# A selection's place in VectorE's queue, and four gates copied out by ScalarE: one Trainium2 core

## The chip, the cores and the metric

The kernel runs on one core of one Trainium2 chip. The metric is the time of one execution in device microseconds; lower is better. Each version is given by the median of several runs, and one further execution of each was profiled.

## The reference, cut to what matters

Two layers over 512 tokens and 1024 channels, all in float32. The part that the change touches is the mixing half of a layer:

```python
h = rms_norm(x); z = h @ w_in           # one projection, its columns shared out:
qa, ka, va, qi, ki, wi, cq, ckv, kr, ga, gb = split_cols(z)
# mixer A: an indexer scores every earlier key, the best 128 of each query are attended
score = einsum(relu(qi . ki), wi);  sel = top_k(score, 128)
y_a = softmax(qa . ka[sel] * scale + bias[sel]) @ va[sel]
# mixer B: latent attention
qb = rms_norm(rope(rms_norm(cq) @ b_w_uq));  kb, vb = from rms_norm(ckv) @ b_w_ukv
y_b = softmax(qb . kb * scale + chunk_mask) @ vb
# merge
gate_a = sigmoid(ga + b_gate[:1024]);  gate_b = sigmoid(gb + b_gate[1024:])
x = x + (gate_a * (y_a @ w_proj_a) + gate_b * (y_b @ w_proj_b)) @ w_out
```

A feed-forward half follows and is not touched.

## The kernel before, in words

Activations lie transposed: channels on the 128 partitions, 512 tokens along the free dimension. Each float32 operand of a product is split into a high part (rounded by ScalarE) and a low part (the difference, mostly by VectorE), and a product is three matmuls. A weight tile of the fixed plan is loaded by SP's queue; ScalarE makes its high part, and its low part comes from VectorE or, for some tiles (gb, ga, kv and uq among them), from a ScalarE copy with the sign turned and an adding DMA on POOL's queue.

**How the order comes about.** The Python program is a set of generators that are advanced in turn. `fl.fill(1)` advances the projections (`mix_dense`) by about three matmuls (a "fill") and moves a clock by one; `later(n, f)` runs `f` when the clock has gone on by n; `flush` runs all that is pending. So the program traces instructions in an order, and this order is their priority. A planner then puts each engine's instructions in a queue at compile time: it goes through time with its own costs and, whenever an engine is free, takes the ready instruction traced earliest. An instruction traced much later, whose inputs are there, can so be placed ahead. On the chip each engine works its queue off in that fixed order. `tc.add_manual_dep(a, b, no_sync)` adds an order to the planner (a behind b) without a semaphore. Tiles are buffers of named pools: PSUM has banks D (2, projections), L (3, mixer B's keys, values, queries and all scores), T (2, transposes), Y (1).

**The stage around the change**, once a layer (layer 0 at about 40 to 340 us of the span, layer 1 at about 800 to 1100):

1. The indexer's queries and keys, then the latents ckv and cq. `index_scores` gives three score tiles `sc` (query blocks 3, 2, 1 with 512, 384, 256 keys).
2. `top_k` (L1036, L1043) on VectorE: 16 rounds. A round takes the 8 largest of each tile (`V.max`, three instructions, one a tile) and strikes them out (`V.match_replace`, three more, each with a short load): 96 steps, each dependent only on steps of its own tile. Three instructions at the end (L1047) write `sel`. POOL adds `sel` to the relative-position bias when mixer A begins (`bias_a`, L1115), and `scores_a` reads the sum (L1134).
3. While `fl.until("b0", side_0)` runs, the fills are gb's gates 0 to 3 (24 matmuls each, eight fills) and then `attn_b(0)`: four blocks of keys and values (L856), four of queries (L893). Each fill is followed by RATE_0 = 1 selection steps. `evac_gate` empties a gate's D bank (L702: `gb = p * row` on VectorE, where `row` is the norm's reciprocal root spread over the tile). Of a value block, ScalarE copies the keys, casts the values and squares the keys, and VectorE makes the values' low part (L315, `vb<-L,vb`): with that the L bank is free. The scaling of the keys (L880) and of the queries (L924) by VectorE comes 22 ticks after their norms, and the transposes (L1149) need it.
4. Mixer B: eight heads, each `scores_b` (VectorE maximum L1167, ScalarE exponential L369), scaling by VectorE (L1063), transposes L1074, products L1081. `each_b` advances the projections meanwhile (`attn_b(1)`, gb 4 to 7, then `attn_a(0)`), and the selection by RATE_T = 0.2 steps a call. What is left of the selection is traced behind mixer B.
5. Mixer A, eight heads, with ga's gates among the fills; then the sigmoids (L369 on gb, ga), the projections pb and pa, and the merge (L944, L1337, L1338).

An option `PK`, off here, tied the first maximum of a round behind the latest gate eviction or row maximum (`tables["v"]`); an option `GBL`, off, had all gb gates copied by ScalarE and multiplied just ahead of the sigmoids.

Of the kernel before, what the change touches and what calls it, by code (L numbers as in the profile page):

```python
# [10 lines left out]
F32 = mybir.dt.float32  # L11
# [4 lines left out]
OP = mybir.AluOpType  # L16
# [23 lines left out]

RATE_B = [0.85, 0.55, 0.75, 0.55]
RATE_A = [0.95, 1.05, 0.65, 0.95]
RATE_T = 0.2
LAG_S = 22
LAG_T = 4
GAP_B = 12
# [6 lines left out]
POOL = ''  # L53
# [9 lines left out]
PBO = 0  # L63
VL = 0
TAIL = 1
TAIL_3 = 3
PK = 0
RATE_0 = 1
DL = ['gb', 'ga', 'uv', 'ug', 'kv', 'uq']
DN1 = []  # L70
DN2 = []
# [3 lines left out]
SU2 = '12'  # L75
PCH = 2000
GA_0 = 0
GBL = 0
LAG_D = [2, 4, 5, 7, 8, 10, 12]
WPOOL = []  # L80
WMOD = 1
# [165 lines left out]
def trunk(ctx: ExitStack, tc: tile.TileContext, xT, wd, vecs, bias, rot_n, outT):  # L247
# [33 lines left out]
    V, A, G = nc.vector, nc.scalar, nc.gpsimd  # L281
# [5 lines left out]
    def later(n, f):  # L287
        if n == 0:
            f()
        else:  # L290
            pending.append((clock[0] + n, f))
# [17 lines left out]
        split_into(h, o, src, scale, lag)  # L309
        return h, o  # L310

    def split_into(h, o, src, scale=None, lag=1):
        if scale is None:
            A.copy(h, src)
            later(lag, lambda: V.tensor_tensor(out=o, in0=src, in1=h.bitcast(F32), op=OP.subtract))  # L315
        else:
            A.activation(h, src, AF.Copy, scale=scale)
            later(lag, lambda: V.scalar_tensor_tensor(o, src, scale, h.bitcast(F32), op0=OP.mult, op1=OP.subtract))
# [45 lines left out]
    no_sync = mybir.DependencyInfo(mybir.DependencyClass.NoSync, mybir.DependencyReason.DATA)  # L364
# [204 lines left out]
    done = set()  # L569
    late = []  # L570

    def mix_dense(l, nrm):
# [122 lines left out]

        def evac_gate(name, m, p):
            g = slot(name)
            if name == "gb" and GBL and not PBO:
                A.copy(g, p)
                late.append((g, nrm.row))  # L700
            else:
                tables["v"] = V.tensor_tensor(out=g, in0=p, in1=nrm.row, op=OP.mult)  # L702
            st[name][m] = g
# [129 lines left out]
        def attn_b(g):  # L833
# [12 lines left out]
            while len(st.get("ckvl", ())) < 2:  # L846
                yield
            h, o = W.get("kv", g)
            for t in range(4):
                ts = slice(t * 128, (t + 1) * 128)  # L850
                p = bank(BB)
                xs = [(st["ckvh"][k][:, ts], st["ckvl"][k][:, ts]) for k in range(2)]
                seq = ([(x, h, k) for k in range(2) for x in xs[k]] + [(xs[k][0], o, k) for k in range(2)] if "k" in LO
                       else [q for k in range(2) for q in ((xs[k][0], h, k), (xs[k][1], h, k), (xs[k][0], o, k))])
                for n, (x, w, k) in enumerate(seq):
                    mm(p, lhsT=x, rhs=w[:, k * 512:(k + 1) * 512], start=n == 0, stop=n == 5, skip_group_check=True)  # L856
                    if n == 2:
                        yield
                if t == 3:
                    W.ahead()  # L860
                p = p.rearrange("p (h c) -> p h c", c=64)
                A.copy(k4[t][:, :, 0:64], p[:, 0:4])
                v = vb[t].rearrange("p (h c) -> p h c", c=128)
                split_into(v[:, :, 0:64], v[:, :, 64:128], p[:, 4:8])
                squares(p[:, 0:4], ssk[:, t], 64)
                yield

            def keys():
                m = small("mk", [4, 4])
                V.tensor_tensor(out=m, in0=ssk, in1=st["sskr"][:, :, None].to_broadcast([128, 4, 4]), op=OP.add)  # L870
                V.tensor_scalar(m, m, 1.0 / 96, EPS, op0=OP.mult, op1=OP.add)
                r = rsqrt(m, [4, 4])

                def scale():
                    for t in range(4):
                        G.tensor_tensor(out=k4[t][:, :, 64:96],
                                        in0=st["kr"][:, t:t + 1, :].to_broadcast([128, 4, 32]),
                                        in1=r[:, t, :, None].to_broadcast([128, 4, 32]), op=OP.mult)
                        G.tensor_copy(k4[t][:, :, 96:100], late_k[:, t:t + 1, :].to_broadcast([128, 4, 4]))
                        (G if "K" in POOL else V).tensor_tensor(out=k4[t][:, :, 0:64], in0=k4[t][:, :, 0:64],  # L880
                                        in1=r[:, t, :, None].to_broadcast([128, 4, 64]), op=OP.mult)
                later(LAG_S, scale)
            later(3, keys)
# [32 lines left out]
            def queries():  # L916
                m = small("mq", [4, 4])
                V.scalar_tensor_tensor(m, ssq, 1.0 / 96, st["epscq"][:, :, None].to_broadcast([128, 4, 4]),
                                       op0=OP.mult, op1=OP.add)
                r = rsqrt(m, [4, 4])  # L920

                def scale():
                    for t in range(4):
                        (G if "Q" in POOL else V).tensor_tensor(out=q4[t][:, :, 0:96], in0=q4[t][:, :, 0:96],  # L924
                                        in1=r[:, t, :, None].to_broadcast([128, 4, 96]), op=OP.mult)
                later(LAG_S, scale)
            later(3, queries)
            st["b", g] = (qn, kn, vb)
# [100 lines left out]
    def top_k():  # L1029
        def low():  # L1030
            return tc.high_priority(offset=-PT) if PT else ExitStack()
        m8 = {i: small("m8", [8]) for i in (1, 2, 3)}
        for _ in range(TOPK // 8):
            for i in (3, 2, 1):
                with low():
                    ins = V.max(out=m8[i], in_=st["sc"][i][:, :128 * (i + 1)])  # L1036
                if PK and i == 3 and "v" in tables:
                    tc.add_manual_dep(ins.ins, tables["v"].ins.name, no_sync, reason="spread")
                yield
            for i in (3, 2, 1):  # L1040
                s = st["sc"][i][:, :128 * (i + 1)]
                with low():
                    V.match_replace(out=s, in_to_replace=m8[i], in_values=s, imm_value=TAKEN)  # L1043
                yield
        for i in (3, 2, 1):
            w = 128 * (i + 1)
            V.tensor_scalar(sel[:, SEL0[i]:SEL0[i] + w], st["sc"][i][:, :w], TAKEN, BIG, op0=OP.not_equal,  # L1047
                            op1=OP.mult)
            yield
# [182 lines left out]
    for l in range(DEPTH):  # L1232
# [10 lines left out]

        fl.fill(GAP_I)
        weave([index_scores()], lambda: fl.fill(1))
        tk = top_k()

        def side_tk(n):
# [6 lines left out]
        due = [0.0]  # L1255

        def side_0():
            due[0] += RATE_0
            side_tk(int(due[0]))
            due[0] %= 1  # L1260

# [4 lines left out]
        def mixer(name, scores, turn, v, each, group):  # L1266
# [6 lines left out]
            for h in range(8):  # L1273
                if h == (3 if turn else 4):
                    fl.until(group + "1")
                    flush()
                each.at(h)
                if turn:
                    P = sb.tile([128, 1280], F32, name=nm("P"), tag="P", bufs=WB[2])
                else:  # L1280
                    P, ahead = (ahead if h else first_a), (bias_a(h + 1) if h < 7 else None)
# [26 lines left out]
                     lambda h: lambda j: st["va"][j][h // 4][:, (h % 4) * 128:(h % 4 + 1) * 128], each_a, "a")  # L1308
        fl.until("ga")
        gb = st["gb"]  # L1310
        for g, row in late:
            V.tensor_tensor(out=g, in0=g, in1=row, op=OP.mult)
        late.clear()
        for m in range(0 if PBO else 8):
            table(AF.Sigmoid, gb[m], gb[m], bias=vc(l, V_GATE + 8 + m))

# [334 lines left out]
```

## Time and profile before

| what | value |
|---|---|
| median of 3 runs | 1537.66 us (1537.4 to 1538.77) |
| the profiled execution | 1536.24 us, its span 1534.5 us |
| busy, share of the span | TensorE 99%, VectorE 73%, ScalarE 62%, POOL 26% |
| granted TensorE clock | 1.00 |
| selection maxima (L1036) | 96, the first at 52.6 us, the last at 929.0 us |
| `sel` written (L1047) | first at 175.1 us, last at 937.3 us |
| gb evictions by VectorE (L702) | 16, median 680 ns |

The page gives busy time and idle time for each engine; idle time of an engine matters only where TensorE waits for it. A row of a group reads: line, engine, operation, tiles out<-in, shapes, xcount, then busy us, mean ns of one, and idle us ahead of it with what ended it. A row by stretch reads: stretch, its length, then busy us and (xcount) of PE, PEld, DVE, ACT, POOL, and at the end clock, DMA share and GB/s; where one line was asked for, only its own engine's number stands there. A row of a tile reads: line, engine, operation, tiles, xcount, shortest/median/longest ns, first and last start.

### The profile page before, as it was taken

The numbers are of one execution on the slowest core, as the hardware profiler recorded it, in microseconds if no ns is written. First come the engines' busy times: TensorE is split into PE (matmuls) and PEld (weight loads), VectorE is DVE, ScalarE is ACT, GpSimd is POOL, SyncE is SP. The second block draws the span as 40 slices with busy tenths as digits, with TensorE's granted clock in tenths as the row PEclk, the third lists the DMA queues.
The fourth block names the chain that finished last, engine by engine and source line by source line (L and its number), as shares of the span: only waits on it lengthen the run. The fifth ranks groups of instructions, "written<-read, shape, count | busy, mean of one in ns | idle before, by whom it ended". The sixth has DMA issues, their size and how long they took to land.

```text
span 1534.5 us, 23946 instructions
## 1 busy us (share of the span) xinstructions
PE 1525.7 (99%) x8658; PEld 1335.7 (87%) x8658; DVE 1124.4 (73%) x2305; ACT 946.3 (62%) x1553; POOL 396.3 (26%) x578
## 2 busy tenths in 40 slices
PE   9999999999999999999999999999999999999999
PEld 8887999888888898889998889998888888988899
DVE  7899988666476693547979999886674857835586
ACT  7756668773577536664557576687635765456642
POOL 2343012400011442124602520223001115311364
PEclk9999999999999999999999999999999999999999
DMA  7464124733488438873454641356436783488732
GB/s 247 108 158 119 53 86 113 190 118 116 128 191 190 104 117 218 194 177 90 152 171 112 159 107 56 104 134 174 129 97 147 182 189 91 149 197 197 181 99 91
DMA packets 73575, 216.29 MB, mean 141 GB/s; under 512 B 8432, under 2 KB 11504, under 8 KB 73456
## 3 DMA queue, kind: packets, MB, share of 16 engines
q1 hardware_dynamic: 54592, 149.08, 30.7%
q0 software_dynamic: 18432, 65.28, 22.8%
q8 instruction: 68, 1.11, 0.3%
q14 instruction: 51, 0.42, 0.1%
q10 hardware_dynamic: 432, 0.40, 0.1%
HBM read 141.06 MB, written 4.19 MB: 95 GB/s over the span
## 4 chain that ended last, share of the span: by engine, by line
PE 86%; DVE 11%; ACT 2%; issue 1%; DMA 0%; SPq 0%; DVEq 0%; ACTq 0%
PE D L535 37%; PE T L535 15%; PE D L558 7%; PE L L1446 5%; PE T L1446 4%; PE D L1446 3%; DVE sc L1043 2%; PE Y L1081 2%; DVE m L1036 2%; PE Y L1446 2%; PE T L1074 2%; PE L L535 2%; PE L L336 1%; PE L L335 1%; PE L L728 1%
## 5 line engine op out<-in xcount | busy, mean ns | idle before, releaser
L182 ACT CAST wh<-wr 128x1024 fp32r<-128x1024 f32 (+2 forms) x205 | 211.3, 1034 | 163.7 <-PE D L535 73.8
L211 POOL DMA_DIRECT2D wl<-wr x128 | 110.7, 874 | 630.2 <-ACT wl L210 591.9
L535 PE MATMUL D<-hxh,wh 128*128 128x512 f32 (+1 forms) x440 | 174.0, 396 | 0.0
L535 PE MATMUL D<-hxl,wh 128*128 128x512 f32 (+1 forms) x440 | 172.8, 393 | 0.0
L210 ACT ACTIVATE wl<-wr 128x1024 fp32r<-128x1024 f32 (+2 forms) x128 | 132.2, 1035 | 48.1 <-PE D L535 25.9
L200 ACT CAST wh<-wr 128x896 fp32r<-128x896 f32 x88 | 82.6, 942 | 102.4 <-POOL wr L224 56.2
L1115 POOL TENSOR_TENSOR P<-M,sel 128x128 f32<-128x128 f32 (+1 forms) x64 | 53.4, 889 | 271.2 <-DMA M<-in_bias_dram 150.2
L535 PE MATMUL D<-hxh,wl 128*128 128x512 f32 (+1 forms) x440 | 117.8, 393 | 0.0
L224 POOL TENSOR_TENSOR wr<-wr 128x256 f32<-128x256 f32 x88 | 101.0, 1151 | 57.9 <-DVE wr L223 41.9
L558 PE MATMUL D<-wh,hxh 128*128 128x256 f32 x384 | 113.8, 297 | 0.0
L205 DVE TENSOR_TENSOR wl<-wr,wh 128x896 fp32r<-128x896 f32 x88 | 101.9, 1161 | 10.2 <-ACT wh L200 4.3
L558 PE MATMUL D<-wl,hxh 128*128 128x256 f32 x384 | 109.3, 285 | 0.0
L558 PE MATMUL D<-wh,hxl 128*128 128x256 f32 x384 | 108.4, 283 | 0.0
L535 PE MATMUL D<-hrl,wh 128*128 128x512 f32 x256 | 99.6, 389 | 0.0
L535 PE MATMUL D<-hrh,wh 128*128 128x512 f32 x256 | 99.6, 389 | 0.0
L535 PE MATMUL T<-hrh,wh 128*128 128x512 f32 x256 | 99.6, 389 | 0.0
L535 PE MATMUL T<-hrl,wh 128*128 128x512 f32 x256 | 99.6, 389 | 0.0
L194 DVE TENSOR_TENSOR wl<-wr,wh 128x1024 fp32r<-128x1024 f32 x77 | 94.9, 1238 | 6.3 <-ACT wh L182 5.6
L535 PEld LDWEIGHTS D<-hxh,wh 128*128 128x128 f32 x440 | 82.9, 188 | 13.4 <-DVE gb L702 0.2
L535 PEld LDWEIGHTS D<-hxl,wh 128*128 128x128 f32 x440 | 82.9, 188 | 12.7
L535 PEld LDWEIGHTS D<-hxh,wl 128*128 128x128 f32 x440 | 80.2, 188 | 14.0
L1390 DVE SCALAR_TENSOR_TENSOR c<-T,vec,c 128x511 f32<-128x511 f32 x32 | 23.9, 748 | 89.1 <-ACT c L1387 89.1
(458 smaller groups left out, 4571.4 us busy)
## 6 DMA issues: line engine op xcount, KB each, us to landing
wr<-in_wd_dram SPq DMA_DIRECT2D x197, 512.0 KB, 3.8
wl<-wr POOLq DMA_DIRECT2D x120, 512.0 KB, 5.4
wr<-in_wd_dram SPq DMA_DIRECT2D x88, 256.0 KB, 2.6
x<-in_xT_dram SPq DMA_DIRECT2D x16, 256.0 KB, 5.2
M<-in_bias_dram SPq DMA_DIRECT2D x16, 256.0 KB, 4.0
wr<-in_wd_dram SPq DMA_DIRECT2D x7, 384.0 KB, 3.2
kah<-kah SPq DMA_DIRECT2D x16, 128.0 KB, 4.3
kal<-kal SPq DMA_DIRECT2D x16, 128.0 KB, 3.8
```

The source lines that it names most:

```text
L182: ins = self.nc.scalar.copy(h[:, :n], t[:, :n])
L194: eng.tensor_tensor(out=o[:, c], in0=t[:, c], in1=h[:, c].bitcast(F32), op=OP.subtract)
L200: self.nc.scalar.copy(h[:, :896], t[:, 128:1024])
L205: self.later(lag, lambda: self.nc.vector.tensor_tensor(out=o[:, :896], in0=t[:, 128:1024], in1=h[:, :896].bitcast(F32), op=OP.subtract))
L210: self.nc.scalar.activation(o, t, AF.Copy, scale=-1.0)
L211: self.nc.gpsimd.dma_start(o.bitcast(F32), t, accum_op=OP.add)
L224: g(2)(out=b[:, 6:8], in0=b[:, 0:3:2], in1=b[:, 3:6:2], op=OP.add)
L535: mm(p[:, t0:], lhsT=w, rhs=x[:, t0:], start=n == 0, stop=n == len(seq) - 1, skip_group_check=True)
L558: mm(pp[b][:, t, :], lhsT=x, rhs=w, start=n == 0 and half == 0 and t == 0, stop=n == 11 and half == 1, skip_group_check=True)
L1036: ins = V.max(out=m8[i], in_=st["sc"][i][:, :128 * (i + 1)])
L1115: G.tensor_tensor(out=P[:, P0[i]:P0[i] + w], in0=M[:, 512 - w:512], in1=sel[:, SEL0[i]:SEL0[i] + w], op=OP.add)
L1446: mm(p, lhsT=w, rhs=x, start=b0, stop=b1, skip_group_check=True)
```

## The change

- The selection (`PK = 1`): every maximum, of all three tiles, is placed behind the latest "hold" traced so far. A hold is the low part of a value block (`split_into(..., last=True)`), a key scaling or a query scaling of mixer B. It is cleared at the start of each layer's selection, so that maxima traced ahead of the first value block are free.
- Its rates: 1.55 steps a fill until the first value weight is taken up (`done.add("values")`), 0.5 from there until group 0 is through, 0.25 a call in mixer B.
- The gates gb 0 to 3 (`GBL = 4`): ScalarE copies the bank as it is; the multiplication with `row` is traced at the start of mixer A's heads 4, 5, 6 and 7, one each, on VectorE in SBUF. It was traced for all ahead of the sigmoids in the old option.

```diff
-RATE_T = 0.2
+RATE_T = 0.25
...
-PK = 0
-RATE_0 = 1
+PK = 1
+RATE_0 = 1.55
+RATE_1 = 0.5
...
-GBL = 0
+GBL = 4
+LATE_H = (4, 5, 6, 7)
...
-    def split_into(h, o, src, scale=None, lag=1):
+    def split_into(h, o, src, scale=None, lag=1, last=False):
         if scale is None:
             A.copy(h, src)
-            later(lag, lambda: V.tensor_tensor(out=o, in0=src, in1=h.bitcast(F32), op=OP.subtract))
+
+            def low():
+                ins = V.tensor_tensor(out=o, in0=src, in1=h.bitcast(F32), op=OP.subtract)
+                if last:
+                    tables["hold"] = ins
+            later(lag, low)
...
-            if name == "gb" and GBL and not PBO:
+            if name == "gb" and m < GBL:
                 A.copy(g, p)
                 late.append((g, nrm.row))
...
             h, o = W.get("kv", g)
+            done.add("values")
...
-                split_into(v[:, :, 0:64], v[:, :, 64:128], p[:, 4:8])
+                split_into(v[:, :, 0:64], v[:, :, 64:128], p[:, 4:8], last=True)
...
-                        (G if "K" in POOL else V).tensor_tensor(out=k4[t][:, :, 0:64], in0=k4[t][:, :, 0:64],
+                        tables["hold"] = V.tensor_tensor(out=k4[t][:, :, 0:64], in0=k4[t][:, :, 0:64],
...
-                        (G if "Q" in POOL else V).tensor_tensor(out=q4[t][:, :, 0:96], in0=q4[t][:, :, 0:96],
-                                        in1=r[:, t, :, None].to_broadcast([128, 4, 96]), op=OP.mult)
+                        tables["hold"] = V.tensor_tensor(
+                            out=q4[t][:, :, 0:96], in0=q4[t][:, :, 0:96], in1=r[:, t, :, None].to_broadcast([128, 4, 96]), op=OP.mult)
...
-                if PK and i == 3 and "v" in tables:
-                    tc.add_manual_dep(ins.ins, tables["v"].ins.name, no_sync, reason="spread")
+                if PK and "hold" in tables:
+                    tc.add_manual_dep(ins.ins, tables["hold"].ins.name, no_sync, reason="spread")
...
+        tables.pop("hold", None)
         tk = top_k()
...
-            due[0] += RATE_0
+            due[0] += RATE_1 if "values" in done else RATE_0
...
                 each.at(h)
+                if not turn and h in LATE_H:
+                    g, row = late.pop(0)
+                    V.tensor_tensor(out=g, in0=g, in1=row, op=OP.mult)
...
-        for g, row in late:
-            V.tensor_tensor(out=g, in0=g, in1=row, op=OP.mult)
-        late.clear()
```

## The prediction

> **What bounds the kernel now.** I read the page's totals first, then busy time by stretch, then what TensorE (PE) waited for, then the order on VectorE (DVE).
>
> ```profile
> span 1534.5 us, 23946 instructions
> PE 1525.7 (99%) x8658; PEld 1335.7 (87%) x8658; DVE 1124.4 (73%) x2305; ACT 946.3 (62%) x1553; POOL 396.3 (26%) x578
> ```
>
> PE is busy nearly throughout, so the change can gain only where PE waits or lose by making it wait: all of PE's idle time is 1534.5 - 1525.7 = 8.8 us. The stretches around the selection, layer 0 and then layer 1 (PE, PEld, DVE, ACT, POOL):
>
> ```profile
> 66.00:92.00 26.00, 26.00 (x121) 21.66 (x120) 26.00 (x76) 11.01 (x16) 5.15 (x7) 1.00 0.56 133
> 92.00:118.00 26.00, 24.59 (x119) 19.87 (x118) 26.00 (x92) 17.57 (x43) 17.89 (x52) 1.00 0.69 167
> 118.00:138.00 20.00, 19.38 (x104) 15.56 (x103) 19.74 (x59) 16.25 (x35) 10.30 (x26) 1.00 0.53 132
> 138.00:176.00 38.00, 37.84 (x254) 33.99 (x253) 37.78 (x91) 24.76 (x59) 0.00 (x0) 1.00 0.21 70
> 176.00:224.00 48.00, 47.57 (x376) 45.75 (x375) 41.96 (x99) 34.77 (x75) 0.00 (x0) 1.00 0.29 89
> 853.00:880.00 27.00, 26.43 (x130) 22.03 (x129) 27.00 (x95) 19.29 (x45) 17.88 (x52) 1.00 0.74 178
> 880.00:900.00 20.00, 19.56 (x107) 15.95 (x106) 20.00 (x64) 17.44 (x36) 10.38 (x26) 1.00 0.51 108
> 900.00:938.00 38.00, 38.00 (x255) 34.58 (x254) 37.40 (x88) 24.98 (x59) 0.00 (x0) 1.00 0.27 83
> 938.00:985.00 47.00, 46.58 (x368) 44.85 (x367) 40.81 (x94) 34.61 (x74) 0.00 (x0) 1.00 0.29 88
> ```
>
> VectorE has no idle time from 66 to 118 and hardly any until 176, and PE idles 1.41 + 0.62 = 2.03 us where mixer B's keys, values and queries are made (92 to 138), 0.57 + 0.44 = 1.01 us in layer 1. The clock is 1.00 everywhere. PE's waits by line and releaser (sum, times, longest): three rows of 92 to 138, two of 853 to 900, and one that fell in 138 to 176:
>
> ```profile
> PE L L856 <- DVE vb L315: 0.8, 2, 0.6
> PE L L1164 <- ACT P L369: 0.6, 1, 0.6
> PE L L893 <- DVE vb L315: 0.5, 1, 0.5
> PE T L1074 <- DVE P L1063: 0.4, 1, 0.4
> PE L L856 <- DVE vb L315: 0.4, 1, 0.4
> PE T L1074 <- DVE tbl L315: 0.2, 1, 0.2
> ```
>
> Four of the six large ones wait for a value eviction (vb). Why that was late stands in VectorE's order, and what a wait costs in PE's (start, duration; the last row is from the chain, 24 matmuls without a wait):
>
> ```profile
> 97.74 0.87 DVE L1036 MAX8 m<-sc 128x8 f32<-128x384 f32 x2
> ...
> 99.26 0.54 DVE L1043 MATCH_REPLACE8 sc<-m,sc 128x384 f32<-128x384 f32 x1
> 99.72 0.41 DVE L315 TENSOR_TENSOR vb<-L,vb 128x256 fp32r<-128x256 f32 x1
> ...
> 107.96 0.39 PE L535 MATMUL D<-hxl,wh 128*128 128x512 f32 x1
> 108.94 0.50 PE L856 MATMUL L<-wh,ckvh 128*128 128x512 f32 x1 [0.59 <-DVE vb L315]
> ...
> 430.52 5.44 PE D L535 x24
> ```
>
> The eviction at 99.72 sits behind 2.0 us of selection, all of it L1036 and L1043 from 97.74 on. The wait shown as 0.59 costs 108.94 - 107.96 - 0.23 (one pitch, 5.44 / 24) = 0.75 us: a shown wait plus 0.16, since a matmul's modelled end lies 0.16 after the next one's start. So the five rows (six waits) cost 0.8 + 0.6 + 0.5 + 0.4 + 0.4 = 2.7, plus 6 x 0.16, together 3.7 us. Idle time that these rows don't list, 2.03 + 1.01 - 2.7, adds 0.3. **At stake: 4.0 us.**
>
> **The tie.** Each selection maximum (L1036) may no longer stand on VectorE ahead of the latest value eviction, key scaling or query scaling traced before it. It adds no instruction and no semaphore: it is an order in VectorE's own queue. What I count along the generators: four gates and a step are 33 fills from the start of the wait for b0 to the first value weight. At 1.55 steps a fill some 50 steps are traced there (33 at rate 1), untied, and with the replacements of that round 54 may run freely. The 16 fills of group 0's values and queries add 8 at 0.5, mixer B's start until group 1's query scaling about 8 more at 0.25. So maxima 55 to 57 come behind group 0's last value eviction, 61 to 63 behind group 1's last one and its key scaling, and from 67 on all wait for group 1's query scaling, which stands at 138 now. So 66 steps are done by then. How many are now:
>
> ```profile
> 92.00:138.00 46.00, 8.34 (x16) 1.00 0.62 152
> 92.00:138.00 46.00, 8.94 (x30) 1.00 0.62 152
> 853.00:900.00 47.00, 10.34 (x19) 1.00 0.64 148
> 853.00:900.00 47.00, 10.93 (x37) 1.00 0.64 148
> 138.00:176.00 38.00, 4.09 (x8) 1.00 0.21 70
> 138.00:176.00 38.00, 5.28 (x18) 1.00 0.21 70
> 900.00:938.00 38.00, 2.44 (x5) 1.00 0.27 83
> 900.00:938.00 38.00, 3.57 (x12) 1.00 0.27 83
> ```
>
> (L1036, then L1043, in each stretch; L1043 has a load and a replacement to a step.) After 138 stand 8 + 9 = 17 steps, after 900 stand 5 + 6 = 11, so of 96 steps 79 and 85 are done ahead, and 79 - 16 - 15 = 48 and 85 - 19 - 18 = 48 when the values begin at 92 and 853. The tie moves 13 and 19 steps behind the query scaling. One step takes (8.34 + 8.94 + 10.34 + 10.93) / (16 + 15 + 19 + 18.5) = 0.563 us, so 7.3 and 10.7 us leave the stretch in which evictions queue. VectorE's load there falls to (45.7 - 7.3) / 46 = 84% and (47 - 10.7) / 47 = 77%. At 87% (41.96 of 48, 176 to 224) PE idled 0.43 us in 48, in waits for other things. I let all of the 4.0 us go; the lower bound is the vb waits of the one stretch with a direct cause, 0.5 + 0.16.
>
> What queues behind a waiting maximum: nothing on a semaphore, but VectorE now stands still where evictions aren't ready, and the selection ends later. In 138 to 176, beside 17 steps, one wait of 0.2 (0.36 in cost) fell to VectorE; layer 1's 11 steps show none. 32 steps more at 0.36 for 28 are 0.4 us, taken as a **loss of 0.4**. The bound of zero is layer 1; the upper end is the slower rival.
>
> **The gates.** Four of the eight gate evictions of a layer leave VectorE (680 ns, L702); ScalarE copies instead and VectorE multiplies in SBUF:
>
> ```profile
> L702 DVE TENSOR_TENSOR gb<-D,row x16: 665/680/694, 74.8 to 924.3; 128x512 f32<-128x512 f32 x16
> L1338 DVE TENSOR_TENSOR ga<-ga,gb x16: 682/686/693, 356.4 to 1138.5; 128x512 f32<-128x512 f32 x16
> L314 ACT CAST pth<-T 128x512 fp32r<-128x512 f32 x16 | 9.3, 582 | 0.4 <-PE T L1074 0.3
> ```
>
> A copy of this size costs ScalarE 582 ns: 4 x 0.58 = 2.3 us into a stretch where it has 26 - 11 = 15 us idle, so nothing, as long as the two D banks (5.44 us of matmuls each, by the chain's row of 24) cover a queue of two weight conversions. VectorE gets 4 x 0.68 = 2.7 us, worth 4.8 steps, so the free 54 are through when the values begin. The multiplication is traced at mixer A's heads 4 to 7, but nothing ties it: its inputs are ready from 75 us on, and the planner may put it into the holes that the tie makes. It costs as much as the eviction did (686 against 680 ns), so VectorE's total doesn't fall. In the crowded stretches 38.6 us of selection (the four numbers above) cost PE at most 4.0 us, 0.10 each. Eight late multiplications there, 5.5 us, would cost 0.6 at that rate; the 5.4 us that leave ahead of the values gain as much, which the 4.0 holds already. I take 0, which is right if the planner leaves them at or near mixer A's heads; bounds -0.6 and +0.6.
>
> The Trainium skill, Perfetto Trace Analysis, section Optimizing Scalar/DVE Operations, gives a VectorE access overhead of about 60 ns in SBUF and 125 ns in PSUM; by it each late multiplication would be an estimated 65 ns cheaper, 0.5 us of VectorE time in eight. The rows above show 686 against 680 ns, no gain, and the sum goes by the rows.
>
> The same PSUM banks, weights, matmuls and DMAs remain. POOL only loses a choice that was off (its list is empty), and neither SP's nor POOL's queue is passed by anything.
>
> **Sum.** -4.0 + 0.4 + 0 = -3.6 us. The profiled execution took 1536.24 us (its span plus 1.7), so it becomes 1532.6; the median of the runs is 1537.66, 1.4 higher, and I forecast **1534.1**.
>
> **Rivals.**
>
> *The wait moves* (same). With VectorE free, the next to be late is ScalarE, which empties the same L banks three times a tile (17.57 of 26 and 19.29 of 27 us busy), or POOL, whose rotations come ahead of the query scaling (17.89 of 26). Or the tie binds too late: VectorE must have passed the 50 untied steps when the first eviction is ready; it stood at 48, and the freed 4.8 steps leave a margin of three. Then half of 4.0 remains: -2.0 + 0.4, 1536.1.
>
> *The selection ends too late* (slower). Mixer A's first bias addition reads its result:
>
> ```profile
> 224.04 7.52 POOL L1115 TENSOR_TENSOR P<-M,sel 128x128 f32<-128x128 f32 x8 [93.69 <-DMA M<-in_bias_dram]
> 985.57 7.52 POOL L1115 TENSOR_TENSOR P<-M,sel 128x128 f32<-128x128 f32 x8 [91.49 <-PE T L1074]
> 230.45 0.28 DVE L1134 CUSTOM_DVE_ANT_0 P<-L,P 128x128 f32<-128x128 f32 x1
> ```
>
> The moved 7.3 + 10.7 = 18.0 us must fit into VectorE's idle time of 138 to 224 and 900 to 985: 0.22 + 6.04 and 0.60 + 6.19, 13.05 us, and half of the 6.4 us between the addition and its first reader, 3.2 a layer. With a share f of the idle time usable, the balance is 18.0 - 13.05 f - 6.4 - 4.0 = 7.6 - 13.05 f: a loss over 3.1 us below f = 0.34, none above 0.58. At f = 0.2 it is +5.0, 1542.7. For it: the order is fixed ahead, and an idle slot goes unused where no step stands. Against: 138 to 176 used 99% beside the selection. The Trainium skill, Perfetto Trace Analysis, section Identifying the Most-Contended Engine, says to speed up the engine with the highest occupancy; VectorE's work stays as it was here, and by that page this rival is the natural outcome.
>
> **How the numbers follow.** 0.2% is 3.1 us, about what a measurement here can tell from nothing. The forecast's case has 0.6 (from -1.5 to -7; 0.43 of it beyond -3.1), the moved wait 0.23 (0.04 beyond), the late selection 0.17 (0.15 beyond +3.1). Faster 0.47, same 0.38, slower 0.15. The range: 1530.5 takes in the 4.0, the 0.16 + 0.43 + 0.42 us of PE's idle time after 138, and 1 us a layer for another order of PE's work (its idle time differs by 1.0 between the layers); 1540.5 reaches halfway into the late selection. The forecast's own range is 1530.5 to 1536.
>
> **What would show it.** PE's rows "L856 <- DVE vb" and "L893 <- DVE vb" gone or under 0.3; fewer than 70 steps ahead of group 1's query scaling; VectorE idle above 5 us in 92 to 138; no gb eviction by L702 for the first four, a ScalarE copy instead; the result of the selection (sel) written at 195 to 225 instead of 175; the first bias addition still at 220 to 225, 985 less the gain in layer 1. I'm wrong if POOL's first addition waits for sel, if new PE waits for VectorE appear in 138 to 224, or if the late multiplications stand directly ahead of vb evictions.

## The result, and the profile after

The changed kernel takes 1547.37 us (median of 6 runs, 1545.47 to 1549.0), the kernel before 1537.75: ratio 1.0062, interval 1.0049 to 1.0075. It is 9.6 us slower where 3.6 us less were forecast. The profiled execution took 1549.0 us (before: 1536.24), so the traces below have to explain 12.8 us, of which 3 are the luck of the two executions. In the new kernel's line numbers the value eviction is L319, the key scaling L888, the query scaling L932, the selection L1044 and L1051, the products L1089, the late multiplication L1289.

```profile
span 1547.3 us, 23946 instructions
PE 1529.6 (99%) x8658; PEld 1335.9 (86%) x8658; DVE 1131.8 (73%) x2305; ACT 950.3 (61%) x1561; POOL 389.1 (25%) x578
```

The same 2305 VectorE instructions take 7.4 us more (1131.8 against 1124.4). Where the time went is seen from the lengths of the stages, each from a first matmul to the next stage's first, so that the work in them is the same: values to the end of mixer B, then mixer A, for both layers. First the kernel before, then the changed one (stretch, length, then busy us of PE, PEld, DVE, ACT, POOL):

```profile
90.30:217.00 126.70, 124.27 (x802) 110.39 (x801) 121.76 (x333) 91.10 (x204) 28.37 (x78) 1.00 0.37 102
217.00:336.90 119.90, 119.72 (x756) 106.52 (x754) 83.33 (x211) 90.93 (x185) 32.57 (x40) 1.00 0.48 131
853.80:978.40 124.60, 123.35 (x803) 110.81 (x802) 119.07 (x328) 92.52 (x205) 28.26 (x78) 1.00 0.39 103
978.40:1098.30 119.90, 119.72 (x755) 106.45 (x754) 83.16 (x211) 91.06 (x185) 33.66 (x40) 1.00 0.49 131
```

```profile
91.20:222.80 131.60, 125.51 (x803) 110.81 (x802) 125.03 (x331) 91.76 (x206) 28.50 (x78) 1.00 0.36 99
222.80:343.70 120.90, 120.04 (x754) 106.36 (x753) 83.17 (x211) 91.08 (x185) 32.75 (x40) 1.00 0.47 129
860.70:989.00 128.30, 124.16 (x803) 110.53 (x801) 122.87 (x325) 93.25 (x206) 26.67 (x78) 1.00 0.38 100
989.00:1111.10 122.10, 120.64 (x755) 106.45 (x754) 85.50 (x211) 91.02 (x185) 33.71 (x40) 1.00 0.49 129
```

The stretch with mixer B grew by 4.9 and 3.7 us, mixer A by 1.0 and 2.2 us. VectorE now stands idle there (131.60 - 125.03 = 6.6 us, 4.9 before), and TensorE waits more, mostly for it:

```profile
PE L L864 <- DVE vb L319: 3.3, 3, 1.2
PE Y L1089 <- DVE ptl L319: 1.9, 5, 0.6
PE L L1172 <- ACT P L376: 1.7, 2, 0.8
PE L L901 <- DVE vb L319: 1.6, 2, 0.8
PE T L800 <- DVE ptl L319: 1.4, 3, 0.7
PE T L1157 <- DVE qn L932: 0.9, 2, 0.5
```

The waits for value evictions, which the change was to remove, went from 1.7 to 4.9 us, and waits for the low parts of the probabilities (ptl), absent before, add 3.3. What stands ahead of the late evictions is in VectorE's order. Here are two places (start, duration):

```profile
93.41 0.41 DVE L1051 MATCH_REPLACE8 sc<-m,sc 128x256 f32<-128x256 f32 x1
93.73 2.49 DVE L1289 TENSOR_TENSOR gb<-gb,row 128x512 f32<-128x512 f32 x4
96.14 0.41 DVE L319 TENSOR_TENSOR vb<-L,vb 128x256 fp32r<-128x256 f32 x1
...
107.66 1.03 DVE L888 TENSOR_TENSOR kn<-kn,y 128x256 f32<-128x256 f32 x2
108.62 0.54 DVE L851 TENSOR_REDUCE ssq<-sqb 128x4 f32<-128x384 f32 x1
109.08 0.73 DVE L888 TENSOR_TENSOR kn<-kn,y 128x256 f32<-128x256 f32 x1
109.74 0.41 DVE L319 TENSOR_TENSOR vb<-L,vb 128x256 fp32r<-128x256 f32 x1
110.07 0.61 DVE L926 SCALAR_TENSOR_TENSOR mq<-ssq,ms 128x16 f32<-128x16 f32 x1
110.61 1.58 DVE L888 TENSOR_TENSOR kn<-kn,y 128x256 f32<-128x256 f32 x1
112.19 0.41 DVE L319 TENSOR_TENSOR vb<-L,vb 128x256 fp32r<-128x256 f32 x1
```

At 93.73 all four late multiplications, traced at mixer A's heads 4 to 7, stand ahead of group 0's first value eviction. At 107.66 three key scalings of group 0 stand ahead of group 1's first value eviction (none before), and the fourth, stretched to 1.58 us, ahead of its second. The tied steps left a hole, and the planner filled it with what was ready. A key scaling cost 0.41 us before; here POOL works beside it:

```profile
L880 DVE TENSOR_TENSOR kn<-kn,y x16: 409/411/547, 108.9 to 885.5; 128x256 f32<-128x256 f32 x16
```

```profile
L888 DVE TENSOR_TENSOR kn<-kn,y x16: 424/617/1585, 107.7 to 893.2; 128x256 f32<-128x256 f32 x16
L1055 DVE TENSOR_SCALAR sel<-sc x6: 263/348/421, 197.2 to 956.7; 128x512 bf16<-128x512 f32 x2, 128x384 bf16<-128x384 f32 x2, 128x256 bf16<-128x256 f32 x2
```

POOL's rotations, 0.32 us when alone, are stretched as well (start, duration):

```profile
106.32 0.31 POOL L919 TENSOR_TENSOR qn<-qn,rot 128x64 f32<-128x64 f32 x1
...
107.81 1.04 POOL L914 TENSOR_TENSOR rot<-qn,rotn 128x64 f32<-128x64 f32 x1
```

By the second row above (`sel`), the first part of the selection's result is written at 197 (in layer 0) and the last at 957 (in layer 1), instead of 175 and 937. That puts the last steps between mixer B's probabilities in its second half:

```profile
195.50 0.67 DVE L1051 MATCH_REPLACE8 sc<-m,sc 128x512 f32<-128x512 f32 x1
...
196.17 0.53 DVE L1051 MATCH_REPLACE8 sc<-m,sc 128x384 f32<-128x384 f32 x1
...
196.69 0.40 DVE L1051 MATCH_REPLACE8 sc<-m,sc 128x256 f32<-128x256 f32 x1
197.02 0.27 DVE L319 TENSOR_TENSOR ptl<-T,pth 128x128 fp32r<-128x128 f32 x1
...
197.35 0.33 PE L1089 MATMUL Y<-ptl,vb 128*128 128x128 f32 x1 [0.37 <-DVE ptl L319]
```

Three replacements, with their loads 1.5 us, stand ahead of the low part that TensorE's product waits for.

### The profile page after: what moved, and what is told of

Read it like the earlier page. It is cut to its first block, busy times and chain, and to the rows that moved or that the text cites. A ratio compares the mean times of both kernels' runs of the same rounds, so it can differ in the third digit from the quotient of the medians.

```text
span 1547.3 us, 23946 instructions
## 1 busy us (share of the span) xinstructions
PE 1529.6 (99%) x8658; PEld 1335.9 (86%) x8658; DVE 1131.8 (73%) x2305; ACT 950.3 (61%) x1561; POOL 389.1 (25%) x578
## 4 chain that ended last, share of the span: by engine, by line
PE 73%; DVE 7%; ACT 2%; issue 1%; DVEq 0%; ACTq 0%
PE D L542 33%; PE T L542 15%; PE L L1455 5%; PE T L1455 4%; PE D L565 3%; PE D L1455 3%; PE Y L1455 2%; PE L L542 2%; PE Y L1089 2%; PE T L1082 1%; DVE sc L1051 1%; DVE m L1044 1%; DVE sc L1032 1%; PE L L343 1%; PE L L342 0%
## 5 line engine op out<-in xcount | busy, mean ns | idle before, releaser
L226 POOL TENSOR_TENSOR wr<-wr 128x256 f32<-128x256 f32 x88 | 93.8, 1069 | 63.0 <-DVE wr L225 51.4
```

The source lines that it names most:

```text
L226: g(2)(out=b[:, 6:8], in0=b[:, 0:3:2], in1=b[:, 3:6:2], op=OP.add)
```

## The experiments

Two quantities from the traces help below. **Excess** is the sum, over the matmuls of a stretch, of the time from one start to the next less the usual time (40th percentile) of a matmul of that shape. **Steps behind** are the selection's maxima and replacements that stand in VectorE's queue behind group 1's last query scaling. Letters of theories are those of the expectation, or of its group, in which they stand. Times are medians of five rounds or more; the kernel before had 1536.96 to 1537.24 in these groups.

**Which part loses.** `e1_tie_alone`: the change without the ScalarE gates, so the tie with its new rates.

```diff
-GBL = 4
-LATE_H = (4, 5, 6, 7)
+GBL = 0
+LATE_H = ()
```

> The tie and its rates, with all gates evicted by VectorE as before the change. Theory H (the tie makes a hole on VectorE, and the late multiplications are planned into it ahead of the value evictions; these cost most of the loss): 2 to 5 us less than the changed kernel, 1542 to 1545. Theory T (the tie itself costs: key scalings and others fill the hole, the queue behind an eviction that is not ready stands still): as slow as the changed kernel, 1546 to 1548. Theory G (the gates' move costs, whatever the tie): as before the change, 1537 to 1539.

1547.52, ratio 1.0070 (1.0059 to 1.0081). `e2_gates_alone`: the gates without the tie, at the old rates (`PK = 0`, `RATE_T = 0.2`, `RATE_0 = RATE_1 = 1`).

> The gates gb 0 to 3 copied by ScalarE and multiplied late, with the selection untied and at its old rates. Theories H and T: no hole, so the late multiplications stand behind the selection; VectorE has 5.4 us less ahead of the values: 1535 to 1538. Theory G: 1542 to 1547.

1539.14, 1.0016 (1.0008 to 1.0025), 2.1 us slower and between the theories' ranges; without the tie's hole the late multiplications stand at 169.7 and later. `e3_rates_alone`: the new rates alone (`PK = 0`, `GBL = 0`).

> The new rates alone: untied, all gates on VectorE. The selection is planned ahead wherever VectorE is free, so its traced rate should matter little: all theories 1536 to 1540. If it is over 1542, the rates are the cause and none of the theories holds.

1539.18, 1.0013 (1.0004 to 1.0021): the rates alone cost 2.1 us. `e4_late_held`: the change, each late multiplication ordered behind the last softmax reciprocal, so that none can be pulled ahead.

```diff
-                    V.tensor_tensor(out=g, in0=g, in1=row, op=OP.mult)
+                    ins = V.tensor_tensor(out=g, in0=g, in1=row, op=OP.mult)
+                    tc.add_manual_dep(ins.ins, tables["end"].ins.name, no_sync, reason="late")
```

> The changed kernel, with each late multiplication placed behind the last softmax reciprocal traced before it on VectorE (mixer A), so that none can be planned ahead. Theory H: 4 to 8 us faster than the changed kernel, 1539 to 1543. Theory T: within 2 us of it, 1545 to 1548. Theory G (the copies by ScalarE cost): 1545 to 1548.

1545.58, 1.0056 (1.0043 to 1.0069): 1.8 us under the change, or 1.1 when each is held against the kernel before of its own group; the intervals overlap. So the tie with its rates, 10.5 us, is the whole loss. What the gates add to it is nothing in sum: by the medians they take 1.9 us off with the multiplications held, and give 1.1 to 1.8 back with them pulled ahead of the values. Without the tie they cost 2.1 us.

**POOL's part, and what holds.** `e8_no_turns` is the tie alone with POOL's six rotation instructions for each query block left out, `e9_before_no_turns` the kernel before with the same left out.

> The tie alone, and POOL's six rotation instructions a query block left out (the queries then carry no rotary turn, a part of the computation). The queues of the other engines stay in the order of the tie alone. Theory P (VectorE's key scalings, planned ahead of group 1's value evictions by the tie, are stretched while POOL works on the same kind of operands, and the evictions wait behind them): the key scalings come down from a mean of 740 ns towards 450, the wait for group 1's value evictions from 3.5 us to under 2, and the time to 1541 to 1545. Theory O (the order alone, whatever POOL does): within 1.5 us of the tie alone, 1546 to 1549.

> The kernel before, with the same rotation instructions left out, to price what their absence does without the tie. Both theories: POOL is off the path there and the key scalings take 411 ns already; 1535.5 to 1537.5.

1541.11 (1.0024, 1.0015 to 1.0033) and 1533.55 (0.9974, 0.9963 to 0.9984): the tie costs 7.6 us without the rotations, 10.5 with them, so some 3 us hang on the rotations. By what way is not shown. The time came into theory P's range, but its signs hardly did: the key scalings went from a mean of 751 ns in `e1_tie_alone` to 657, not towards 450, and their median stayed (616 and 614 ns), for POOL's own part of the keys (L884) still runs beside them. `e9_before_no_turns` is faster than either theory had it. `e6_values_only`: the tie alone, with only value evictions as holds. `e5_keys_behind`: `e4_late_held` with each key scaling ordered behind the latest value eviction.

```diff
-                        tables["hold"] = V.tensor_tensor(out=k4[t]...
+                        V.tensor_tensor(out=k4[t]...
...
-                        tables["hold"] = V.tensor_tensor(
-                            out=q4[t]...
+                        V.tensor_tensor(
+                            out=q4[t]...
```

> The tie alone, but a hold is set by value evictions only, not by key and query scalings; the three key scalings still stand ahead of group 1's first eviction, while the selection flows again behind its last (67 steps, not 64, ahead of group 1's key scaling). Theories P and O: 1545 to 1548, like the tie alone. Theory S: 3 us less or more, 1540 to 1544.

> The changed kernel with the late multiplications held in mixer A (as in e4) and each key scaling placed on VectorE behind the latest value eviction traced, so that no scaling stands ahead of group 1's evictions. Theories P and O: the waits of 1.3 and 1.0 us a layer for those evictions go, 3 to 5 us less than e4, 1540.5 to 1543. Theory S (what costs is the selection's tail in mixer B and what it shifts in mixer A): 1544 to 1546.

1542.0 (1.0028, 1.0017 to 1.0039) and 1544.5 (1.0046, 1.0032 to 1.0060). With values as the only holds the tail is shorter (23 and 17 steps behind, against 30 and 24), and 5.5 us of 10.5 come back, although three key scalings still stand ahead of group 1's first value in both layers. `e5_keys_behind` has none there, and no wait for a value eviction is left in its list of TensorE's waits, but with the full tail it is only 1.1 us faster than `e4_late_held`, as theory S had it.

**Misses.** `e7_scalings_only`: only the scalings hold. `e10_group0`: only group 0's values hold, at the old rates (`last=g == 0`). `e11_tie_short` and `e12_before_short`: the tie alone and the kernel before, with the selection's last five rounds left out (`range(TOPK // 8 - 5)`).

> The tie alone (no ScalarE gates), with the hold set by the key and query scalings and not by the value evictions: the counterpart of e6_values_only. Theory S (the selection steps that are held behind the scalings come too late and get in the way of mixer B's second half and of mixer A) has the 5.5 us that e6 lost here: 1542 to 1544, and the waits of the second half of mixer B are as in e1. Theory P (the hole in front of the value evictions is filled with key scalings, so value evictions come late) has 1538 to 1540, since nothing is held behind a value eviction, and the two parts add up to e1's 10.5 us only if they are independent.

> The tie behind group 0's value evictions only, the former rates, all gates on VectorE as before. Theories P and S: no selection step is held behind anything of group 1, and no key scaling of group 0 gets ahead of group 1's values by it: 1536 to 1539. A rival, that any new order of TensorE's queue costs some us whatever is tied, has 1543 to 1548, since more of TensorE's instructions (259) change their place against the kernel before than in the change itself (229).

> The tie alone with the last five of the selection's sixteen rounds left out: 66 of 96 steps remain, all of which can stand ahead of group 1's query scaling, so that no tail is left behind it. To be held against e12_before_short. Theory S: the difference between the two falls from 10.5 to 4 to 6 us, and the excess time of mixer B's second half (3.0 and 1.7 us in e1, 0.8 and 0.8 before) falls to 0.8. Theory P alone: the difference stays at 8 to 11, since the evictions are late by key scalings, not by the tail.

> The kernel before with the last five of the selection's sixteen rounds left out: the other half of the pair with e11_tie_short. 30 steps a layer less, some 17 us of VectorE time a layer, of which the crowded stretches cost TensorE at most 0.10 us per us of selection: 1534 to 1537. If the crowding of VectorE by the selection itself were the cost, as the prediction held (4.0 us at stake), it would be 1533 to 1535.

1548.73 (1.0075, 1.0063 to 1.0088), 1544.38 (1.0045, 1.0031 to 1.0058), 1541.59 (1.0028, 1.0017 to 1.0039), 1540.94 (1.0027, 1.0015 to 1.0038). With no tail the tie costs 0.65 us more than no tie. That goes theory S's way, though further than its 4 to 6, and the pair is not clean (below). `e7_scalings_only` was expected at 1544 or less and is about as slow as `e1_tie_alone`. It has the same tail, and a hold on values is not needed for early key scalings: in layer 0 all four of group 0 stand ahead of group 1's first value, in layer 1 one, which takes 3.04 us. `e10_group0` was expected at 1536 to 1539. Its trace says why: at the old rates few steps are free ahead of the values, so 35 and 29 steps stand behind. It writes the first part of `sel` at 222 and the last at 981, its key scalings are not stretched and not early, and its waits are the tail's:

```profile
L888 DVE TENSOR_TENSOR kn<-kn,y x16: 407/414/417, 111.3 to 888.8; 128x256 f32<-128x256 f32 x16
L1055 DVE TENSOR_SCALAR sel<-sc x6: 277/350/426, 222.4 to 981.3; 128x512 bf16<-128x512 f32 x2, 128x384 bf16<-128x384 f32 x2, 128x256 bf16<-128x256 f32 x2
```

```profile
PE T L800 <- DVE ptl L319: 2.1, 4, 0.7
PE Y L1089 <- DVE ptl L319: 1.1, 3, 0.4
...
PE L L864 <- DVE vb L319: 0.6, 2, 0.4
```

And `e12_before_short` is slower than the kernel it takes 60 steps from. There the hole comes without a tie: one and two key scalings stand ahead of group 1's first value, and they go up to 1177 ns. Its excess in the stage of keys, values and queries rises from 3.3 and 2.1 us to 4.1 and 4.2; another 2.8 us lie ahead of layer 0's values (their first matmul starts at 93.1, not 90.3), in no single wait, and stay unexplained. Its profiled execution is also 2.1 us above its median.

**Key scalings and tail apart.** `e16_keys_after`: the kernel before, group 0's key scalings ordered behind group 1's third value. `e17_keys_first`: the kernel before, group 1's first value behind group 0's third key scaling. `e15_tail_alone`: only group 1's query scaling holds, new rates. `e10b_group0`: `e10_group0` with the new rates.

```diff
# e16_keys_after (value = the latest low part with t <= 2), no other tie
+                        tc.add_manual_dep(ks.ins, tables["value"].ins.name, no_sync, reason="keys")
# e17_keys_first (value = the low part with t == 0)
+                        if g == 0 and t == 2:
+                            tc.add_manual_dep(tables["value"].ins, ks.ins.name, no_sync, reason="keys")
# e15_tail_alone
+                        if g == 1:
+                            tables["hold"] = ins
```

> The kernel before, with no tie and no ScalarE gates; group 0's four key scalings are ordered behind group 1's third value eviction, nothing else is moved (four VectorE instructions change their place, none of TensorE's). Theory P (key scalings ahead of value evictions cost TensorE its waits in the stage of keys, values and queries): the excess time of that stage goes from 3.27 and 2.05 us to the 2.2 and 1.7 of e10_group0, which has the same order of these eight instructions: 1535.5 to 1536.5. Theory S (selection steps left for mixer B's second half cost there and in mixer A) and theory N (any new order of TensorE's queue costs, some 0.03 us for an instruction moved, by e10_group0's 7.4 us for 259): no change, 1537.

> The kernel before, with no tie; group 1's first value eviction is ordered behind group 0's third key scaling, so that two key scalings stand ahead of it (three in the changed kernel, none before). The selection keeps its places (17 and 12 steps behind group 1's query scaling, against 17 and 11). Theory P: the stage of keys, values and queries goes from 3.27 and 2.05 us of excess to 4 to 5 and 3 to 4, mixer B's second half stays at 0.8: 1539 to 1541. Theory S: no change, 1537. Theory N: 75 of TensorE's instructions moved, 1539.

> The tie with group 1's query scaling as the only instruction that holds: 30 and 24 steps are left behind it (17 and 11 before), as in the changed kernel. In layer 1 the key scalings and value evictions keep the order of before; in layer 0 two key scalings come ahead of group 1's values. Theory S: the second half of mixer B goes from 0.8 and 0.8 us of excess to 3 and 1.7, mixer A from 2.4 to 3.5 to 5, 1542 to 1544; layer 1's stage of keys and values stays at 2 to 2.5 us. Theory P: only layer 0's stage of keys and values grows, 1538 to 1539. Theory N: 192 moved, 1543, spread over all stages.

> e10_group0 with the new rates: the tie behind group 0's values alone, 52 and 56 steps free ahead of them, 23 and 14 left behind group 1's query scaling (35 and 29 in e10_group0, 17 and 11 before), the key scalings where they stood before. Theory S: of e10_group0's 7.4 us some 2 to 3 remain, in mixer B's second half and mixer A of layer 0: 1538.5 to 1540. Theory P: no change against before, 1537. Theory N: 138 moved, 1541.

1537.1 (1.0000, 0.9992 to 1.0009), 1537.12 (1.0001, 0.9992 to 1.0010), 1543.59 (1.0045, 1.0032 to 1.0058), 1539.07 (1.0011, 1.0003 to 1.0020). The key scalings' order alone is worth nothing either way: in `e17_keys_first` one or two stand ahead of group 1's first value, but at 412 ns in the median, so this does not price stretched ones. The tail alone, at the new rates, costs 6.6 us. Shortened (`e10b_group0`, 23 and 14 steps) it costs 2.1, which is what the new rates cost without any tie. Theory N, a price on any new order, is not borne out as stated: 75 moved TensorE instructions cost nothing.

`e18_tail_keys` is `e15_tail_alone` with the key scalings as in `e16_keys_after`; `e19_tie_keys` is `e1_tie_alone` with the same.

> e15_tail_alone with group 0's four key scalings ordered behind group 1's third value eviction (three of TensorE's instructions change their place against e15_tail_alone). Both layers then have the late tail (30 and 24 steps behind group 1's query scaling) without a key scaling ahead of the values that stood behind them before: the tail by itself. Theory S: mixer B's second half stays at 2 to 3 and 1.7 to 2.5 us of excess, the whole at 1542 to 1543.5. If early key scalings count too (what is left of theory P), layer 0's stage of keys and values falls from 4.1 to 2.5 to 3.3 us: 1542 to 1542.8.

> The tie alone (e1_tie_alone), with group 0's four key scalings ordered behind group 1's third value eviction; the tail is as long as in e1_tie_alone (30 and 24 steps). What is left of theory P (three key scalings ahead of group 1's first value, stretched to 0.5 to 1.6 us there by POOL's work, cost the 3 to 4 us by which e1_tie_alone is slower than e15_tail_alone): the stage of keys and values goes from 4.5 us in layer 0 and 3.8 in the changed kernel's layer 1 to 2.2 to 3, and the time from 1547.5 to 1543.5 to 1544.5. Theory S alone: the tail is the same and the time stays at 1546.5 to 1548.

1543.54 (1.0040, 1.0028 to 1.0053) and 1543.23 (1.0041, 1.0028 to 1.0055). With the same tail, taking the key scalings from ahead of group 1's values takes the tie from 1547.52 to 1543.23; for the tail alone it changes nothing. Rows of `e19_tie_keys`: key scalings, waits for value evictions, and the four stages:

```profile
L890 DVE TENSOR_TENSOR kn<-kn,y x16: 409/416/542, 111.6 to 888.4; 128x256 f32<-128x256 f32 x16
```

```profile
PE L L866 <- DVE vb L319: 0.5, 2, 0.3
```

```profile
90.60:219.50 128.90, 125.38 (x803) 110.82 (x802) 123.90 (x333) 91.53 (x205) 26.69 (x78) 1.00 0.38 101
219.50:339.60 120.10, 119.75 (x754) 106.32 (x753) 82.22 (x211) 90.94 (x185) 33.28 (x40) 1.00 0.48 130
857.00:985.00 128.00, 124.38 (x802) 110.36 (x801) 121.70 (x328) 92.17 (x205) 27.84 (x79) 1.00 0.38 101
985.00:1105.10 120.10, 119.92 (x756) 106.64 (x754) 83.43 (x211) 91.00 (x185) 33.75 (x40) 1.00 0.49 131
```

Value evictions are no longer late (0.5 us, less than the kernel before), mixer A is back at 120.1, and what is left, 2.2 and 3.4 us, lies in the stretch with mixer B.

A late eviction can also cost more than its wait. In layer 1 of `e1_tie_alone` two key scalings take 3.50 us beside POOL's rotations, TensorE waits 3.33 us for the value behind them, and the clock granted to it is 0.50 for 6.8 us (two rows by start and duration, then the row of the stretch):

```profile
875.76 3.50 DVE L888 TENSOR_TENSOR kn<-kn,y 128x256 f32<-128x256 f32 x2
880.44 0.79 PE L864 MATMUL L<-wh,ckvh 128*128 128x512 f32 x1 [3.33 <-DVE vb L319]
879.50:886.30 6.80, 5.86 (x16) 5.28 (x17) 5.60 (x24) 2.82 (x5) 1.59 (x5) 0.50 0.51 154
```

By an estimate from this row, half of 6.8 us, 3.4, is lost in such a stretch. `e7_scalings_only` (a wait of 2.74 us, then 0.50 for 3.4 us) and `e17_keys_first` (1.91, then 0.51) show the same at this place; a wait of 2.00 us at 109.8 in `e1_tie_alone` was not followed by it, so no threshold is shown. In the profiled execution of the changed kernel the longest of these waits is 1.16 us and the clock stays at 1.00. But its mean clock is 0.999 in three of six runs, and under 1.000 in four of six of `e1_tie_alone`, against 1.000 in every run of `e19_tie_keys` and every run of the kernel before whose clock is listed. So a part of what those runs lost goes with the clock.

In mixer B the tail can be read as a dose. Steps that run in mixer B's second half (by time), and TensorE's excess in that half, layer 0 and layer 1:

| kernel | steps, excess us | steps, excess us |
|---|---|---|
| before | 8, 0.81 | 4, 0.80 |
| before, five rounds left out | 0, 0.78 | 0, 0.81 |
| e10b_group0 | 13, 1.89 | 7, 0.87 |
| e6_values_only | 13, 1.55 | 9, 0.81 |
| after | 17, 3.02 | 13, 1.66 |
| e15_tail_alone | 18, 2.24 | 14, 2.46 |
| e10_group0 | 25, 3.07 | 21, 3.18 |

Up to nine steps cost nothing in that half; 13 and more cost 0.7 to 2.4 us a layer (in `e8_no_turns` 11 steps go with 1.67). No kernel with a short tail has more than 0.9 there, however its order differs.

So the 10.5 us have two parts. **6.0 to 6.6 us go with the late tail at the new rates** (`e19_tie_keys`, `e18_tail_keys`, `e15_tail_alone`). The rates alone cost 2.1 of that, which leaves 3.9 to 4.5 for the tail if the two add up; that a tail costs without them is shown by `e10_group0`, 7.4 us at the old rates. Only about half lies in mixer B's second half (`e15_tail_alone`: 2.24 + 2.46 - 0.81 - 0.80 = 3.1 us of excess); the rest is spread over the stages ahead of it.

**Up to 4.3 us go with key scalings that fill the hole** ahead of group 1's values (`e1_tie_alone` less `e19_tie_keys`), stretched beside POOL's work, and with the clock behind long waits. That size is not exact: a like order in the changed kernel with its multiplications held (`e5_keys_behind` against `e4_late_held`) got only 1.1 us back. No version tried with the whole computation beats the kernel before; the nearest are `e16_keys_after` and `e17_keys_first`, equal to it.

## Why the prediction was wrong

The count was right where it could be followed: in layer 0, 66 steps are done when group 1's query scaling comes (72 in layer 1, where 66 were expected), and 13 more than before stand behind it in each layer, as forecast for layer 0 (19 were forecast for layer 1).

- **"I let all of the 4.0 us go"** is the step that failed. It took a VectorE with a lower load to be an earlier VectorE. The stretch did get idle time, but the waits for vb went from 1.7 to 4.9 us. The place of a selection step ahead of an eviction was not left empty: the planner put ready key scalings and gate multiplications there. The prediction's own text described such a planner, and applied it to the late multiplications alone, not to the key scalings. That the filling made the evictions late is shown by `e19_tie_keys`, where the waits for vb fall to 0.5 us. Yet even there nothing of the 4.0 is gained: the excess in the stage of keys, values and queries is 5.7 us in both layers together (5.3 before). The least that any run of the whole computation has there is 4.0 (`e10_group0`).
- **The "loss of 0.4" for 32 more steps** is the term that was mis-sized: with the new rates, for which the sum has no term, it is 6.0 to 6.6 us, and without their 2.1 some 4. It scaled the price of a step from 138 to 176, where 17 steps stood beside one wait of 0.36 us. The moved steps landed later: the first half of mixer B kept its number (16 and 16 before, 15 and 15 after), the second half went from 8 and 4 to 17 and 13, and there the same number is dear: waits for ptl, and of the transposes of mixer A's queries (L800) for ptl, are new in the profile. The row of 176 to 224, 0.43 us of idle time in 48 at 87%, was measured where no step stood.
- **The gates at 0** held for the sum by luck, through two errors that cancel: -1.9 us with the multiplications held (`e4_late_held` against `e1_tie_alone`), +1.1 to 1.8 with them pulled ahead. Both are larger than the bounds of 0.6, though neither is beyond the runs' intervals. Without the tie the gates cost 2.1 us (`e2_gates_alone`), and there the interval leaves out zero.
- **The rival "the selection ends too late"** had the right sign and the wrong place. It let the selection press on mixer A's first bias addition; in layer 0 that starts at 229.9 after waiting for ptl, not for sel, long after sel's first part at 197. Its +5.0 us stand near the tail's cost by accident. Nor is VectorE, at 73%, the busiest engine, as that rival takes it; TensorE is, at 99%. The **rival "the wait moves"** appears in one row (L1172 <- ACT P, 0.6 to 1.7 us).
- The signs named as fatal came: new waits for VectorE between 138 and 224, and late multiplications directly ahead of vb.

Not settled: why mixer A grew by 1.0 and 2.2 us. In layer 1 three waits for ptl fall there, one behind three scalings of probabilities that run beside POOL's bias addition:

```profile
1046.77 3.12 POOL L1123 TENSOR_TENSOR P<-M,sel 128x128 f32<-128x128 f32 x4 [13.48 <-DMA M<-in_bias_dram]
...
1047.65 2.46 DVE L1071 TENSOR_SCALAR P<-P,rs 128x128 f32<-128x128 f32 x3
1050.50 0.38 PE L1089 MATMUL Y<-ptl,va 128*128 128x256 f32 x1 [0.61 <-DVE ptl L319]
```

In `e15_tail_alone` and `e19_tie_keys` mixer A is as before. But it is 1.3 and 1.6 us longer in `e10_group0`, which has no early key scalings, and 0.9 and 1.7 in `e17_keys_first`, which has no tie and whose profiled execution is 5.2 us above its median. So the growth follows neither part by itself, and luck of the profiled execution (1.6 us above the median here) is not ruled out. The 2.1 us of the new rates alone, with not one of TensorE's instructions moved, have no shown cause either; their trace has 1.2 us more excess in layer 1's stage of keys, values and queries, where one key scaling takes 1.19 us.

## What to carry to other kernels

Taking an instruction from ahead of a critical one in a planned queue helps only if nothing else that is ready may take its place: before tying one thing back, list what the planner would take next, and tie that too or leave the filler where it is. Price deferred work by the stage in which it lands and what queues behind it there, not by what it cost in another stage. And a late eviction's cost is seen in what stands ahead of it in the queue, not in the engine's busy share, which fell here (121.76 of 126.70 us before, 125.03 of 131.60 after) while the waits grew.

## What the runs showed of the hardware

- A VectorE product of two SBUF operands (128x256) takes 411 ns alone and 0.6 to 1.6 us beside POOL's work in the changed kernel, up to 3.1 us in `e1_tie_alone`. The Trainium skill, SBUF — State Buffer, section Who interferes with whom, says that a VectorE instruction with two SBUF inputs contends with a GpSimd instruction that reads SBUF. The rows agree, on both sides: POOL's rotation went from 0.32 to 1.04 us. Three scalings of probabilities, of 128 columns and more and with one tensor as input, which that sentence does not cover, took 0.86 us where POOL rests (from 194.31) and 2.46 beside a bias addition.
- After waits of 1.91, 2.74 and 3.33 us of TensorE in layer 1 its granted clock was half for 3.4, 3.4 and 6.8 us (`e17_keys_first`, `e7_scalings_only`, `e1_tie_alone`); after one of 2.00 us in layer 0 it was not.
- Leaving out POOL's rotations makes the kernel before 3.6 us faster (`e9_before_no_turns`), though POOL is busy for only a quarter of the span.
- Fewer instructions can be slower: 60 selection steps less cost 4.0 us (`e12_before_short`).
